# Storing the output by tokens instead of by features, and starting the streamed rows 40 bytes later: one decoder step on one core

## The chip, the core and the metric

One core of a Trainium2 chip runs one inference step of a hybrid decoder layer: 256 prompt tokens and 8 sample tokens go through the same weights in float32. TensorE (PE in the profile) multiplies; its weight loads are shown apart as PEld. VectorE is DVE, ScalarE is ACT, GpSimd is POOL, and SyncE (SP) issues most of the transfers. The metric is the time of one execution on the device in microseconds (us); lower is better.

## The reference

What is computed, cut to what this change touches:

```python
hn = rmsnorm(h, norm_gain)                  # h: 264 tokens (256 + 8) x 4096
P  = hn @ w_in                              # one projection, its columns split into groups
A  = sliding_window_attention(...) * silu(z_a)
B  = mlstm(...)  -> also the states C, n, m
C  = u * (tril(W_s) v + b) * silu(z_c)
h  = h + concat(A, B, C) @ w_out            # 4096 x 4096
y  = h * rsqrt(mean(h*h, -1) + 1e-6) * final_gain
```

The outputs are y for the 256 prompt tokens and for the 8 sample tokens, the new rows of keys and values, and the states.

## The kernel before

Activations lie with features on the 128 partitions and tokens along the row. The 4096 features are `KT` = 32 blocks of 128, the 264 tokens are `T`. `yb` [128, 32, 264] holds the input at first, later the gated mixer outputs, later still the residual and the output.

A float32 product is made from three passes at full precision of the array's fast format: the streamed operand is split into `xh` + `xl`, the weights into `wh` + `wl` (tiles [128, 2, 512], three buffers each), and each block adds `wh·xh`, `wh·xl` and `wl·xh` in PSUM. The streamed operand is always a row of `xh` or `xl`, 264 numbers of 4 bytes. Rows of `xh` and `xl` are `ROW` = 320 numbers (1280 bytes) apart, and both tiles start at an address that is a multiple of 256 bytes, so every row starts at such a multiple; so do the weight tiles.

The main loop walks `steps`, pairs of a group (26 groups of 512 columns of `w_in`, then `NGO` = 8 groups of `w_out`) and one of 16 chunks of two feature blocks. Each step issues a 512 KB weight load four steps ahead (SP's queue), the split of the weights two steps ahead (ACT makes `wh`, DVE `wl`), and 24 matmuls, so a group has 384 and the program 13,056. The schedule is written out by hand: each engine executes its instructions in the order in which the code emits them. Small work of the mixers runs in generators between the matmuls.

After a group of `w_out`, `evac_out(i, ps)` adds the product of output block i to `yb` (DVE), squares it (ACT), adds the square to `acc` (POOL, for all but the last two blocks, which stay apart in the list `last`), and multiplies the block by its column of `final_gain` (ACT).

The tail begins after the last matmul. `state_mm(h)` computes the state of head h in PSUM (two matmuls), `state_out(h)` copies it to `co` (ACT), and three transfers on ACT's queue store it as `o_cp`. `norm_factor` sums the squares over the partitions with an all-ones matrix, so the factor `rstd` appears on all 128 partitions for all 264 tokens: ACT takes the root, and DVE does a reciprocal and three more operations, all [128, 264]. `finish` then multiplies 32 blocks of `yb` by `rstd`, every fourth one on POOL, the others on DVE, and SP stores them with nine transfers as `o_y` [128, 32, 264], features on the partitions.

PSUM is split into pools: `pm` with four buffers (tile `mp`: the main products, and the states in the tail), `px` with three (`mx`), `pn` with one.

Of the kernel before, what the change touches and what calls it, by code (L numbers as in the profile page):

```python
# [10 lines left out]
F32 = mybir.dt.float32  # L11
F32R = mybir.dt.float32r
AF = mybir.ActivationFunctionType
ALU = mybir.AluOpType
# [4 lines left out]
P = 128  # L19
D = 4096  # L20
KT = D // P
TP = 256
TS = 8
T = TP + TS
AH, AKV = 12, 4
MH, DK, DV = 6, 128, 256
# [39 lines left out]
NGO = 8  # L66
# [3 lines left out]
LAG = 6.0  # L70
NCH = KT // KK
ROW = 320
PAD0, PAD1 = 32, 24

SM = {}
# [13 lines left out]


def body(tc, xt, wi, wg, wo, sm, kc, vc, c0, wst, w00, bs, cgain, cbias,
         o_y, o_kv, o_cp, o_mp, o_cs, o_ms, o_cvp, o_cvs):
    nc = tc.nc
    from contextlib import ExitStack
    with ExitStack() as ctx:
        cp = ctx.enter_context(tc.tile_pool(name="const", bufs=1))
        wp = ctx.enter_context(tc.tile_pool(name="wp", bufs=3))
        hp = ctx.enter_context(tc.tile_pool(name="hp", bufs=1))
        dp = ctx.enter_context(tc.tile_pool(name="dp", bufs=1, space=DRAM))
        pm = ctx.enter_context(tc.tile_pool(name="pm", bufs=8 - 1 - NMX, space=PSUM))  # L100
        px = ctx.enter_context(tc.tile_pool(name="px", bufs=NMX, space=PSUM))
        pn = ctx.enter_context(tc.tile_pool(name="pn", bufs=1, space=PSUM))
# [20 lines left out]
        ph = Phase("ph")  # L123
# [1 line left out]
        keep = Phase("keep")  # L125

        cp.tile([P, PAD0], F32, name="pad0")
        xh = cp.tile([P, KT, ROW], F32R, name="xh")[:, :, :T]
        xl = cp.tile([P, KT, ROW], F32R, name="xl")[:, :, :T]
        yb = cp.tile([P, KT, T], F32, name="yb")  # L130
        sms = cp.tile([P, NSM], F32, name="sms")
        ones = cp.tile([P, P], F32, name="ones")
        epsc = cp.tile([P, 2], F32, name="epsc")
        epsc2 = cp.tile([P, 1], F32, name="epsc2")
        rstd = cp.tile([P, T], F32, name="rstd")
        cp.tile([P, PAD1], F32, name="pad1")
        acc = cp.tile([P, KK, T], F32, name="acc")

        def sc(name, i=0, n=None, rows=slice(None)):
            o, w = SM[name]  # L140
            return sms[rows, o + i:o + i + (1 if n is None else n)]
# [9 lines left out]
        def tt(eng, out, a, b, op):  # L151
            eng.tensor_tensor(out, a, b, op)
# [56 lines left out]
        V = Eng(nc.vector, "V", 0.1, 0.00104)  # L209
        A = Eng(nc.scalar, "A", 0.25, 0.00083)  # L210
        G = Eng(nc.gpsimd, "G", 0.15, 0.00228)
        PE = Eng(nc.tensor, "P", 0.0, 0.0)
        DQ = nc.sync
# [62 lines left out]
        def newton(out, v, t):  # L276
            V.reciprocal(out, t)
            tt(V, v, v, out, ALU.mult)
            tt(V, v, v, out, ALU.mult)
            V.scalar_tensor_tensor(out, v, 1.5, out, ALU.add, ALU.mult)  # L280

        def norm_factor(ps, parts):
            for i, a in enumerate(parts):
                PE.matmul(ps[:, :T], ones, a, start=(i == 0), stop=(i == len(parts) - 1))
            v = hp.tile([P, T], F32, name="es", bufs=2)
            t = hp.tile([P, T], F32, name="es", bufs=2)

            A.activation(t, ps[:, :T], AF.Sqrt, scale=1.0 / D, bias=epsc[:, 0:1])
            A.activation(v, ps[:, :T], AF.Identity, scale=-0.5 / D, bias=epsc[:, 1:2])
            newton(rstd, v, t)  # L290
# [361 lines left out]
        def attn_sample_loads():  # L652
            Kc = ph.tile([P, TS, AKV, P], F32, name="Kc", tag="big", bufs=2)
            Vc = ph.tile([P, TS, AKV, P], F32, name="Vc", tag="big", bufs=2)

            def loads():
                for dst, src in ((Kc, kc), (Vc, vc)):
                    for i in range(0, TS, 2):
                        DQ.dma_start(dst[:, i:i + 2], src[:, i:i + 2])
                        yield 4.0  # L660

            spawn(loads(), urgent)
            pad = ph.tile([P, TS, AKV, 32], F32, name="pad")
            prod = ph.tile([P, AKV, 32], F32, name="prod")
            G.memset(pad, 0.0)
            G.memset(prod, 0.0)
            st.update(Kc=Kc, Vc=Vc, pad=pad, prod=prod)
# [258 lines left out]
        def before_group(g):  # L926
            if g < NG:
# [14 lines left out]
                if x == ("aq", 0, O_AQ):  # L942
                    attn_sample_loads()

        def evac_out(i, ps):
            y = yb[:, i]
            tt(V, y, ps, y, ALU.add)
            if i >= KT - 2:
                s = hp.tile([P, T], F32, name="et", bufs=4) if i < KT - 1 else acc[:, 1]
                A.activation(s, y, AF.Square)  # L950
                last.append(s)
            elif i == 0:
                A.activation(acc[:, 0], y, AF.Square)
            else:
                s = hp.tile([P, T], F32, name="es", bufs=2)
                A.activation(s, y, AF.Square)
                tt(G, acc[:, 0], acc[:, 0], s, ALU.add)
            A.activation(y, y, AF.Copy, scale=sc("fg", i))
            if i == 0:
                A.activation(epsc2, epsc[:, 0:1], AF.Sqrt)  # L960

        last = []
# [30 lines left out]
        for n, (g, c) in enumerate(steps):  # L993
# [24 lines left out]
            for j in range(4):  # L1018
                tick()
                out = main_ps[j][:, :T]  # L1020
                for kk in range(KK):
                    k = KK * c + kk
                    s = slice(P * j, P * j + P)
                    PE.matmul(out, wh[:, kk, s], xh[:, k], start=(k == 0), stop=False)
                    PE.matmul(out, wh[:, kk, s], xl[:, k], start=False, stop=False)
                    PE.matmul(out, wl[:, kk, s], xh[:, k], start=False, stop=(k == KT - 1))
                if c == NCH - 1:
                    if g < NG:
                        kind, i, _ = GROUPS[g][j]
                        evac(g, kind, i, out)  # L1030
                    else:
                        evac_out(4 * (g - NG) + j, out)
# [14 lines left out]
        ph.close()  # L1047
        ph.switch()
        co = ph.tile([P, MH, DV + 1], F32, name="co")
        cps = []  # L1050

        def state_mm(h):
            ps = pm.tile([P, 512], F32, name="mp")
            for b in range(2):
                PE.matmul(ps[:, :DV + 1], st["kws"][:, h, b], st["va"][:, h, b], start=(b == 0), stop=(b == 1))
            cps.append(ps)

        def state_out(h):
            A.activation(co[:, h], cps[h][:, :DV + 1], AF.Copy)
            if h in (2, 4, 5):  # L1060
                i = {2: 0, 4: 3, 5: 5}[h]
                nc.scalar.dma_start(o_cp[i:h + 1].rearrange("h p d -> p h d"), co[:, i:h + 1])

        state_mm(0)
        norm_factor(px.tile([P, 512], F32, name="mx"), [acc[:, 0]] + last)
        for h in range(MH):
            if h:
                state_mm(h)
            state_out(h)

        def finish(i, m, sl):
            for k in range(i, i + m):
                tt(G if k % 4 == 3 else V, yb[:, k, sl], yb[:, k, sl], rstd[:, sl], ALU.mult)
            DQ.dma_start(o_y[:, i:i + m, sl], yb[:, i:i + m, sl])

        i = 0
        for m in (2, 4, 4, 4, 4, 4, 4, 4, 2):
            finish(i, m, slice(0, T))
            i += m
        ph.close()  # L1080
        keep.close()


_OUTS = {
    "o_y": (P, KT, T), "o_kv": (2, P, AKV, P + TS), "o_cp": (MH, P, DV + 1), "o_mp": (MH, 1),
    "o_cs": (MH, P, TS, DV + 1), "o_ms": (MH, TS), "o_cvp": (P, 1024), "o_cvs": (TS, 1024),
}

# [91 lines left out]
```

## Time and profile before

| what | value |
|---|---|
| time, median of 3 runs | 1690.13 us (1689.64 to 1691.94) |
| the profiled execution's own time | 1690.53 us |
| its span, first to last instruction | 1687.7 us |
| PE busy | 1663.3 us, 99% of the span |
| DVE, ACT, POOL busy | 911.6, 739.1, 80.9 us |
| moved by DMA | 328.91 MB, 195 GB/s over the span |
| last main matmul starts | 1662.66 us after the span's start |

A line of the profile gives the source line, the engine, the operation, output and inputs by the program's names, shapes, the count, and then busy time and mean duration. All compute instructions of this kernel pass through one helper, so they share one line (L205) and are told apart by the names of their tiles. A matmul's shown duration is longer than the distance to the next one, since matmuls overlap in the array; the rate is read from how many fit in a stretch. A row of a view over stretches ("windows") gives, for each engine, the busy time and in brackets the number of instructions seen in it, then the granted clock of TensorE, the busy share of the 16 DMA engines and the rate.

### The profile page before, as it was taken

To read this page: it belongs to the slowest core of one execution; us is meant where nothing else is said; L and a number is where in the kernel's file an instruction comes from. 1 tells how busy PE (TensorE), PEld (TensorE's weight loads), DVE (VectorE), ACT (ScalarE), POOL (GpSimd) and SP (SyncE) were. 2 spreads that over 40 slices of the span, in tenths; PEclk is the share of its full clock that TensorE was granted. 3 is DMA by queue.
4 is the path that set the end of the run, shared out by engine and by line. 5 is a ranking of instruction groups with operands and counts; after the bars stand their busy time and mean duration, and the time that the engine had idled before them with its cause. 6 is when DMAs were issued, how large, how long until landed. Compare 5 with 4: busy or idle time off the path is not lost.

```text
span 1687.7 us, 32534 instructions
## 1 busy us (share of the span) xinstructions
PE 1663.3 (99%) x13754; PEld 1646.4 (98%) x13754; DVE 911.6 (54%) x1277; ACT 739.1 (44%) x971; POOL 80.9 (5%) x82
## 2 busy tenths in 40 slices
PE   9999999999999999999999999999999999999995
PEld 9999999999999999999999999999999999999995
DVE  6565644555544455556665666444666554444445
ACT  6554433444434343444444444334454444344442
POOL 0000000000000000001001100000100030000002
PEclk9999999999999999999999999999999999999998
DMA  8555568545455555667767666555656656555553
GB/s 297 172 181 178 184 191 278 157 156 165 151 173 178 184 179 184 205 205 234 229 215 241 216 226 214 185 179 185 204 176 224 203 192 192 187 180 184 180 182 147
DMA packets 102177, 328.91 MB, mean 195 GB/s; under 512 B 11090, under 2 KB 24328, under 8 KB 102032
## 3 DMA queue, kind: packets, MB, share of 16 engines
q1 hardware_dynamic: 101072, 326.04, 60.4%
q8 instruction: 107, 1.75, 0.4%
q10 hardware_dynamic: 960, 0.81, 0.1%
q14 instruction: 38, 0.31, 0.0%
HBM read 314.20 MB, written 12.60 MB: 194 GB/s over the span
## 4 chain that ended last, share of the span: by engine, by line
PE 96%; DVE 2%; DMA 1%; ACT 1%; issue 0%; SPq 0%; DVEq 0%; ACTq 0%
PE mp L205 92%; PE mx L205 3%; DVE wl L205 1%; DVE yb L205 1%; DMA wf<-wo 1%; PE sn L205 0%; ACT wh L205 0%; DMA wf<-wi 0%; PE gps L205 0%; DVE rstd L205 0%; DVE TM L205 0%; ACT es L205 0%; DVE mvs L205 0%; ACT L205 0%; ACT yb L205 0%
## 5 line engine op out<-in xcount | busy, mean ns | idle before, releaser
L205 PE MATMUL mp<-xh,wh 128*128 128x264 f32 x4352 | 1242.5, 286 | 2.5 <-ACT wh L205 1.9
L205 PE MATMUL mp<-xh,wl 128*128 128x264 f32 x4352 | 1231.3, 283 | 2.6 <-DVE wl L205 2.5
L205 PE MATMUL mp<-xl,wh 128*128 128x264 f32 x4352 | 1230.9, 283 | 0.0
L205 DVE TENSOR_TENSOR wl<-wf,wh 128x1024 fp32r<-128x1024 f32 (+1 forms) x545 | 685.3, 1261 | 741.1 <-ACT wh L205 734.5
L205 ACT ACTIVATE wh<-wf 128x1024 fp32r<-128x1024 f32 (+1 forms) x545 | 574.9, 1057 | 808.6 <-PE mp L205 712.1
L205 PEld LDWEIGHTS mp<-xh,wh 128*128 128x128 f32 x4352 | 819.0, 188 | 9.3 <-issue 5.6
L205 PEld LDWEIGHTS mp<-xh,wl 128*128 128x128 f32 x4352 | 819.0, 188 | 3.9 <-DVE wl L205 3.9
L205 PEld LDWEIGHTS mp<-xl,wh 128*128 128x128 f32 x4352 | 819.2, 188 | 0.4
L205 POOL TENSOR_TENSOR acc<-acc,es 128x264 f32<-128x264 f32 x29 | 21.9, 756 | 412.4 <-ACT es L205 410.3
L205 ACT ACT_TABLE_LOAD x22 | 28.2, 1283 | 1.2 <-PEq L1160 0.8
L205 POOL TENSOR_SCALAR_AFFINE_SELECT tmp<-bc 128x128 f32<-128x128 f32 x12 | 5.1, 448 | 491.8 <-DMA bc<-gd 446.0
L205 ACT ACTIVATE es<-yb 128x264 f32<-128x264 f32 x37 | 15.2, 412 | 17.7 <-DVE yb L205 17.7
L205 POOL TENSOR_TENSOR cb<-cb,bc 128x2056 f32<-128x2056 f32 x6 | 22.5, 3748 | 0.2 <-PE mx L205 0.2
L205 ACT ACTIVATE bias<-bias,ar 128x128 f32<-128x128 f32 (+1 forms) x24 | 10.7, 448 | 24.9 <-DVE ar L205 24.8
L205 POOL MEMSET pad<- 128x1024 f32 x2 | 1.9, 950 | 409.5 <-PE mx L205 409.5
L205 ACT ACTIVATE es<-et 128x264 f32<-128x264 f32 x32 | 12.6, 419 | 17.1 <-DVE yb L205 13.8
L205 DVE SCALAR_TENSOR_TENSOR cb<-vb,wsk,cb 128x257 f32<-128x257 f32 x48 | 20.1, 481 | 0.0
L205 ACT ACTIVATE xh<-yb 128x264 fp32r<-128x264 f32 x32 | 12.1, 412 | 17.7 <-DVE yb L205 17.7
L205 DVE TENSOR_TENSOR et<-mp,rstd 128x264 f32<-128x264 f32 x52 | 18.8, 424 | 0.0
L205 ACT ACTIVATE yb<-yb,sms 128x264 f32<-128x264 f32 x32 | 16.5, 517 | 1.0
L205 DVE TENSOR_TENSOR yb<-yb,rstd 128x264 f32<-128x264 f32 x32 | 16.1, 559 | 0.0
L205 DVE TENSOR_TENSOR xl<-yb,xh 128x264 fp32r<-128x264 f32 x32 | 12.7, 429 | 3.9 <-ACT xh L205 3.9
(177 smaller groups left out, 467.4 us busy)
## 6 DMA issues: line engine op xcount, KB each, us to landing
wf<-wi SPq DMA_DIRECT2D x415, 512.0 KB, 3.4
wf<-wo SPq DMA_DIRECT2D x128, 512.0 KB, 3.4
cb<-c SPq DMA_DIRECT2D x12, 514.0 KB
o_cs<-cb SPq DMA_DIRECT2D x12, 514.0 KB, 6.3
vb<-vsd SPq DMA_DIRECT2D x12, 512.0 KB, 4.6
yb<-xt SPq DMA_DIRECT2D x34, 132.0 KB, 3.4
yb<-xt SPq DMA_DIRECT2D x15, 264.0 KB, 7.3
o_y<-yb SPq DMA_DIRECT2D x7, 528.0 KB, 3.2
```

The costliest lines, as they stand in the source:

```text
L205: return fn(*a, **k)
```

## The change

Three things change, two of them in the tail.

1. `xh` and `xl` keep their addresses and their pitch, but the 264 numbers now begin 10 numbers (40 bytes) into each row of 320.
2. The norm factor is computed by tokens. For each of the two blocks of 128 tokens, the squares are the stationary operand and one column of ones is streamed, so the sum of a token lands on that token's partition; for the 8 sample tokens the factor stays along the row, as before. One small tile of 10 columns replaces the [128, 264] chain.
3. The output is turned. `turn(q, b)` transposes four feature blocks of token block b in PSUM, [128 tokens, 512 features]. `put(q, b)` multiplies the block by the factor of its token while it leaves PSUM, on ACT for b = 0 and on DVE for b = 1, and SP stores it as 128 rows of 2 KB in `o_y` [2, 128, 4096]. The eight sample tokens go out by one DVE operation and one transfer, `o_ys`. POOL has no part any more. The states move to the pool `px`, and their matmuls, copies and transfers (now three of two heads) are dealt between the turned blocks. Since a block must have its `final_gain` before it is turned, that multiplication of the last three blocks comes later: block 29 after the last square, blocks 30 and 31 between the first turned blocks.

```diff
+XOFF = 10
...
-        xh = cp.tile([P, KT, ROW], F32R, name="xh")[:, :, :T]
-        xl = cp.tile([P, KT, ROW], F32R, name="xl")[:, :, :T]
+        xh = cp.tile([P, KT, ROW], F32R, name="xh")[:, :, XOFF:XOFF + T]
+        xl = cp.tile([P, KT, ROW], F32R, name="xl")[:, :, XOFF:XOFF + T]
...
+        def final_gain(k):
+            A.activation(yb[:, k], yb[:, k], AF.Copy, scale=sc("fg", k))
...
-            A.activation(y, y, AF.Copy, scale=sc("fg", i))
+            if i < KT - 3:
+                final_gain(i)
+            elif i == KT - 1:
+                final_gain(KT - 3)
...
+        def state(h):
+            ps = px.tile([P, 512], F32, name="mx")
...
-        norm_factor(px.tile([P, 512], F32, name="mx"), [acc[:, 0]] + last)
...
-        def finish(i, m, sl):
-            for k in range(i, i + m):
-                tt(G if k % 4 == 3 else V, yb[:, k, sl], yb[:, k, sl], rstd[:, sl], ALU.mult)
-            DQ.dma_start(o_y[:, i:i + m, sl], yb[:, i:i + m, sl])
...
+        def turn(q, b):
+            ps = pm.tile([P, 512], F32, name="mp")
+            for k in range(4):
+                tr(ps[:, P * k:P * k + P], yb[:, 4 * q + k, P * b:P * b + P])
+            turned[q, b] = ps
+        def put(q, b):
+            ps, o = turned.pop((q, b)), yo[:, q, b]
+            if b == 0:
+                A.activation(o, ps, AF.Copy, scale=r[:, 0:1])
+            else:
+                V.tensor_scalar(o, ps, r[:, 1:2], None, ALU.mult)
+            DQ.dma_start(o_y[b, :, 512 * q:512 * q + 512], o)
...
+            for b in range(2):
+                PE.matmul(ns[:, b:b + 1], a[:, P * b:P * b + P], ones[:, 0:1], ...)
+            PE.matmul(ns[:, 2:2 + TS], ones, a[:, TP:], ...)
...
+        rsqrt(r[:, 0], ns[:, :2 + TS], 1.0 / D, r[:, 1], r[:, 2])
...
+        for q in range(NGO):
+            put(q, 0)
+            put(q, 1)
+            if q < MH:
+                state_out(q)
+            if q < 2:
+                final_gain(KT - 2 + q)
+            if q == 2:
+                tt(V, yos, yb[:, :, TP:], rs.unsqueeze(1).broadcast_to([P, KT, TS]), ALU.mult)
+                DQ.dma_start(o_ys, yos)
+            if q + 1 < MH:
+                state(q + 1)
+            if q + 2 < NGO:
+                turn(q + 2, 0)
+                turn(q + 2, 1)
```

How the order on two engines changes in the tail. PE before, from the last matmul of the main loop on (`mp<-va,kws` are states, `ones` against `acc` and `et` is the norm):

```order
L205 MATMUL mp<-xh,wl 128x264
L205 MATMUL mp<-va,kws 128x257 x2
L205 MATMUL mx<-acc,ones 128x264
L205 MATMUL mx<-et,ones 128x264
L205 MATMUL mx<-acc,ones 128x264
L205 MATMUL mp<-va,kws 128x257 x10
```

PE after, the same place (`mp<-sms,yb` are the transposes, whose identity matrix lies in `sms`; the norm is the `ns` rows):

```order
L206 MATMUL mp<-xh,wl 128x264
L206 MATMUL mp<-sms,yb 128x128 x8
L206 MATMUL mx<-va,kws 128x257 x2
L206 MATMUL ns<-ones,acc 128x1 x2
L206 MATMUL ns<-acc,ones 128x8
L206 MATMUL ns<-ones,et 128x1 x2
L206 MATMUL ns<-et,ones 128x8
L206 MATMUL ns<-ones,acc 128x1 x2
L206 MATMUL ns<-acc,ones 128x8
L206 MATMUL mp<-sms,yb 128x128 x8
L206 MATMUL mx<-va,kws 128x257 x2
L206 MATMUL mp<-sms,yb 128x128 x8
```

Eight transposes and nine narrow norm matmuls now stand where three wide norm matmuls stood, and the remaining states alternate with further transposes, 64 of these in all.

ACT before, from the last squares on (`et` and `acc` are the squares of blocks 30 and 31, `yb<-yb,sms` is the final gain):

```order
L205 ACTIVATE et<-yb 128x264
L205 ACTIVATE yb<-yb,sms 128x264
L205 ACTIVATE acc<-yb 128x264
L205 ACTIVATE yb<-yb,sms 128x264
L205 ACTIVATE es<-mx,epsc 128x264 x2
L205 ACTIVATE co<-mp 128x257 x3
L1062 DMA o_cp<-co 128x3x257
```

ACT after, the same place:

```order
L206 ACTIVATE et<-yb 128x264
L206 ACTIVATE acc<-yb 128x264
L206 ACTIVATE yb<-yb,sms 128x264
L206 ACTIVATE rn<-ns,epsc 128x10
L206 ACTIVATE yo<-mp,rn 128x512
L206 ACTIVATE co<-mx 128x257
L206 ACTIVATE yb<-yb,sms 128x264
L206 ACTIVATE yo<-mp,rn 128x512
L206 ACTIVATE co<-mx 128x257
L1070 DMA o_cp<-co 128x2x257
```

The last square no longer stands behind a gain, and ACT now carries eight `yo` blocks between the state copies and two late gains.

More of the change, by code (lines that the diff above doesn't have):

```diff
@@ L91, in body @@
 def body(tc, xt, wi, wg, wo, sm, kc, vc, c0, wst, w00, bs, cgain, cbias,
-         o_y, o_kv, o_cp, o_mp, o_cs, o_ms, o_cvp, o_cvs):
+         o_y, o_ys, o_kv, o_cp, o_mp, o_cs, o_ms, o_cvp, o_cvs):
     nc = tc.nc
@@ L1049, in body @@
         co = ph.tile([P, MH, DV + 1], F32, name="co")
-        cps = []
-        def state_mm(h):
-            ps = pm.tile([P, 512], F32, name="mp")
+        yo = ph.tile([P, NGO, 2, 512], F32, name="yo")
+        yos = ph.tile([P, KT, TS], F32, name="yos")
+        turned, cps = {}, {}
+        def state(h):
+            ps = px.tile([P, 512], F32, name="mx")
+            cps[h] = ps
             for b in range(2):
                 PE.matmul(ps[:, :DV + 1], st["kws"][:, h, b], st["va"][:, h, b], start=(b == 0), stop=(b == 1))
-            cps.append(ps)
@@ L1058, in state_out @@
         def state_out(h):
             A.activation(co[:, h], cps[h][:, :DV + 1], AF.Copy)
[L1060 to L1064, printed above, removed]
-        norm_factor(px.tile([P, 512], F32, name="mx"), [acc[:, 0]] + last)
[L1066 to L1069, printed above, removed]
-        def finish(i, m, sl):
-            for k in range(i, i + m):
-                tt(G if k % 4 == 3 else V, yb[:, k, sl], yb[:, k, sl], rstd[:, sl], ALU.mult)
-            DQ.dma_start(o_y[:, i:i + m, sl], yb[:, i:i + m, sl])
@@ L1076, in body @@
[L1076 to L1079, printed above, removed]
+            if h in (1, 3, 5):
+                nc.scalar.dma_start(o_cp[h - 1:h + 1].rearrange("h p d -> p h d"), co[:, h - 1:h + 1])
+        def turn(q, b):
[10 more added lines that the diff above has]
+            DQ.dma_start(o_y[b, :, 512 * q:512 * q + 512], o)
@@ new lines, in body @@
+        turn(0, 0)
+        turn(0, 1)
+        state(0)
+        ns = pn.tile([P, 512], F32, name="ns", tag="sn")
+        parts = [acc[:, 0]] + last
+        for i, a in enumerate(parts):
+            end = i == len(parts) - 1
+            for b in range(2):
+                PE.matmul(ns[:, b:b + 1], a[:, P * b:P * b + P], ones[:, 0:1], start=(i == 0 and b == 0), stop=end,
+                          skip_group_check=True)
+            PE.matmul(ns[:, 2:2 + TS], ones, a[:, TP:], start=False, stop=end, skip_group_check=True)
@@ new lines, in body @@
+        r = hp.tile([P, 3, 2 + TS], F32, name="rn")
+        rsqrt(r[:, 0], ns[:, :2 + TS], 1.0 / D, r[:, 1], r[:, 2])
+        rs = r[:, 0, 2:]
+        r = r[:, 0]
+        turn(1, 0)
+        turn(1, 1)
+        for q in range(NGO):
[13 more added lines that the diff above has]
+                turn(q + 2, 1)
@@ L1084 @@
 _OUTS = {
-    "o_y": (P, KT, T), "o_kv": (2, P, AKV, P + TS), "o_cp": (MH, P, DV + 1), "o_mp": (MH, 1),
+    "o_y": (2, P, D), "o_ys": (P, KT, TS), "o_kv": (2, P, AKV, P + TS), "o_cp": (MH, P, DV + 1), "o_mp": (MH, 1),
     "o_cs": (MH, P, TS, DV + 1), "o_ms": (MH, TS), "o_cvp": (P, 1024), "o_cvs": (TS, 1024),
@@ L1168 @@
     r = _run(nc, [arrays], core_ids=[0]).results[0]
-    y = r["o_y"].transpose(2, 1, 0).reshape(T, D)
+    y, ys = r["o_y"].reshape(TP, D), r["o_ys"].transpose(2, 1, 0).reshape(TS, D)
     kv = r["o_kv"].transpose(0, 3, 2, 1)
@@ L1172 @@
     return (
-        y[:TP].reshape(1, TP, D), y[TP:].reshape(TS, 1, D),
+        y.reshape(1, TP, D), ys.reshape(TS, 1, D),
         kv[0, :P][None, None], kv[1, :P][None, None],
```

## The prediction

> **What bounds the kernel now.** I read the page first, then the chain of waits, then counts of matmuls in long stretches of the main loop, then the tail instruction by instruction.
>
> ```profile
> span 1687.7 us, 32534 instructions
> PE 1663.3 (99%) x13754; PEld 1646.4 (98%) x13754; DVE 911.6 (54%) x1277; ACT 739.1 (44%) x971; POOL 80.9 (5%) x82
> PE 96%; DVE 2%; DMA 1%; ACT 1%; issue 0%; SPq 0%; DVEq 0%; ACTq 0%
> L205 PE MATMUL mp<-xh,wh 128*128 128x264 f32 x4352 | 1242.5, 286 | 2.5 <-ACT wh L205 1.9
> ...
> L205 PE MATMUL mp<-xh,wl 128*128 128x264 f32 x4352 | 1231.3, 283 | 2.6 <-DVE wl L205 2.5
> L205 PE MATMUL mp<-xl,wh 128*128 128x264 f32 x4352 | 1230.9, 283 | 0.0
> ```
>
> PE carries 96% of the chain that ended last, nearly all of it three groups of 4352 matmuls whose streamed operand is a row of `xh` or `xl`; they wait 5 us in all. So two things can move the time: the distance between those 13,056 matmuls, and the tail, 25 us from the last main matmul (1662.66) to the end. The distance comes from counting (columns: stretch, its length, PE busy and count, PEld, DVE, ACT, POOL, clock, DMA share, GB/s):
>
> ```profile
> 507.00:599.00 92.00, 92.00 (x760) 92.00 (x759) 40.66 (x37) 36.02 (x40) 0.00 (x0) 1.00 0.59 183
> 61.00:108.00 47.00, 47.00 (x394) 47.00 (x393) 28.06 (x30) 25.45 (x34) 0.00 (x0) 1.00 0.56 173
> 1139.00:1184.00 45.00, 45.00 (x373) 45.00 (x373) 20.82 (x20) 18.68 (x21) 0.00 (x0) 1.00 0.59 185
> 1478.00:1518.00 40.00, 40.00 (x335) 40.00 (x335) 17.09 (x15) 17.55 (x22) 2.67 (x4) 1.00 0.58 183
> 1431.00:1471.00 40.00, 40.00 (x332) 40.00 (x332) 17.45 (x16) 17.54 (x21) 3.03 (x4) 1.00 0.59 185
> ```
>
> About two of each count began before the stretch. That leaves 92.00/758 = 121.4 ns in the first, 45.00/371 = 121.3 and 40.00/330 = 121.2 in the third and fifth, but 47.00/392 = 119.9 and 40.00/333 = 120.1 in the second and fourth: the same instructions on the same rows run in two rhythms, whole stretches long, at full clock, whatever DVE and ACT do beside them. I take half the matmuls for each. Now the tail:
>
> ```profile
> 1662.66 0.29 PE L205 MATMUL mp<-xh,wl 128*128 128x264 f32 x1
> 1662.79 1.03 PE L205 MATMUL mp<-va,kws 128*128 128x257 f32 x4
> 1663.66 0.62 PE L205 MATMUL mx<-acc,ones 128*128 128x264 f32 x2
> 1664.11 0.61 PE L205 MATMUL mx<-et,ones 128*128 128x264 f32 x2
> 1664.56 0.61 PE L205 MATMUL mx<-acc,ones 128*128 128x264 f32 x2
> 1665.00 4.51 PE L205 MATMUL mp<-va,kws 128*128 128x257 f32 x20
> 1663.93 0.41 ACT L205 ACTIVATE acc<-yb 128x264 f32<-128x264 f32 x1
> 1665.78 1.80 DVE L205 RECIPROCAL rstd<-es 128x264 f32<-128x264 f32 x1 [2.35 <-ACT es L205]
> 1669.09 12.69 DVE L205 TENSOR_TENSOR yb<-yb,rstd 128x264 f32<-128x264 f32 x24
> 1669.13 7.20 POOL L205 TENSOR_TENSOR yb<-yb,rstd 128x264 f32<-128x264 f32 x8 [5.62 <-DVE rstd L205]
> 1670.44 12.64 SPq L1074 DMA_DIRECT2D o_y<-yb  x9
> 1669.00:1672.00 3.00, 0.51 (x3) 0.11 (x1) 2.97 (x5) 0.45 (x2) 2.87 (x4) 1.00 0.75 271
> 1672.00:1677.00 5.00, 0.00 (x0) 0.00 (x0) 5.00 (x8) 0.00 (x0) 4.34 (x5) 0.74 0.29 118
> 1677.00:1685.00 8.00, 0.00 (x0) 0.00 (x0) 4.78 (x14) 0.00 (x0) 0.00 (x0) 0.50 1.01 402
> 1685.00:1687.70 2.70, 0.00 (x0) 0.00 (x0) 0.00 (x0) 0.00 (x0) 0.00 (x0) 0.50 0.26 99
> ```
>
> The factor is ready when the 24 DVE products begin, 1669.09. While POOL multiplies too, DVE manages 8 in 5 us and the transfers stand at a share of 0.29; once POOL is done they run full, 402 GB/s from 1677 to 1685. So the store is fed too slowly for five microseconds and is then its own bound. From 1677.0 on 8.00 x 402 + 2.70 x 99 GB/s = 3.48 MB moved; at 402 GB/s these end 8.7 us later, at 1685.7, so the end follows the last full transfer by 2.0 us.
>
> **The change, part by part.** *Norm.* PE after the last main matmul (its successor starts at 1662.79) first does eight transposes, one state and then the norm:
>
> ```profile
> 818.92 0.60 PE L205 MATMUL mx<-sms,hn 128*128 128x128 f32 x4
> 819.27 0.37 PE L205 MATMUL mp<-xh,wh 128*128 128x264 f32 x1
> 451.86 0.38 PE L205 MATMUL mx<-ones,prod 128*128 128x1 f32 x2
> 452.11 0.37 PE L205 MATMUL mp<-xh,wh 128*128 128x264 f32 x1
> L205 DVE RECIPROCAL r<-r 128x2 f32<-128x2 f32 x12 | 2.0, 166 | 2.0 <-ACT r L205 1.8
> L205 DVE TENSOR_TENSOR r<-r 128x2 f32<-128x2 f32 x18 | 2.9, 162 | 0.6
> L205 ACT ACTIVATE r<-r,epsc 128x2 f32<-128x2 f32 x6 | 1.8, 295 | 0.1
> L205 ACT ACTIVATE va<-mx 128x512 f32<-128x512 f32 x6 | 3.5, 580 | 0.0
> L205 DVE TENSOR_SCALAR hn<-mx,r 128x256 f32<-128x256 f32 x12 | 5.3, 480 | 0.2
> L205 DVE TENSOR_SCALAR kws<-mx,E 128x128 f32<-128x128 f32 x12 | 3.6, 339 | 0.0
> ```
>
> Four transposes take the array 0.44 us at most (the next matmul starts 0.35 behind the first, overlapping the last), so eight take 0.87: 1663.66. A state takes 0.87 (four passes, 1662.79 to 1663.66 above): 1664.53. The squares of block 31 were done at 1664.34 and come 0.44 sooner, without the gain ahead of them, so they don't hold the norm. Its nine matmuls are two passes each; the 128x1 pair took 0.25 with what followed, so nine take 2.25: 1666.8, and 0.2 for the result to come out, 1667.0. In the chain behind, small operations replace wide ones: a root of 0.30, a reciprocal of 0.17, three of 0.16, and 0.1 to cross engines twice: 1668.1, against 1669.09. One us is won, though PE's part is 1.7 us later than now.
>
> *Blocks.* `put` on ACT costs 0.58, as `va<-mx` of the same shape; on DVE, from 0.34 at 128 and 0.48 at 256 columns, 0.76 at 512. ACT has eight of these (4.6), six state copies of 0.39, two gains of 0.52 and three transfer issues of about 0.4:
>
> ```profile
> 1667.35 0.40 ACTq L1062 DMA_DIRECT2D o_cp<-co  x1
> 1667.81 0.39 ACT L205 ACTIVATE co<-mp 128x257 f32<-128x257 f32 x1 [0.49 <-PE mp L205]
> 1664.37 0.52 ACT L205 ACTIVATE yb<-yb,sms 128x264 f32<-128x264 f32 x1
> o_y<-yb SPq DMA_DIRECT2D x7, 528.0 KB, 3.2
> ```
>
> That is 9.2 us; PE has 14 turns of 0.44 and five states of 0.87, 10.5 us, from 1667.0; DVE 6.1 and 0.5 for the sample tokens (256 columns). A turn must wait until a `put` two rounds back frees one of four PSUM buffers, so PE and ACT hold each other up a little: the last block is ready near 1679. POOL's 7.2 us go, and with them the slow five microseconds of DVE.
>
> *Store.* Bytes: `o_y` 4.19 MB, `o_ys` 0.13, `o_cp` 0.79, in all 5.12 MB, 12.7 us at 402 GB/s. Today `o_cp` is out of the way before `o_y` flows; now it shares the flow. First block ready at 1668.7; issue and start of the flow lie between 0 and 1.9 us behind it (3.2 us from issue to landing, less 1.3 for 528 KB at that rate), I take 1.1: 1669.8. 12.7 us later is 1682.5, later than the last block at 1679, so the store bounds; with the 2.0 us behind it the span ends at 1684.5, **3.2 us sooner**. Bounds: flow at once and never starved, 1683.5 (4.2 sooner); turn, `put` and state of a round one after the other, 0.87 + 0.76 + 0.87 + 0.2 = 2.7 us for eight rounds from 1668.1, and 3.2 to land, 1692.9 (5 us later). I take the first kind, since different engines do them. SP issues 17 transfers instead of 9 at 0.33 us each; only themselves wait behind them. The rows stored become shorter, 2 KB instead of 4.2, which may cost rate: from 1669 to 1672, when `o_cp` with 1 KB rows and the first 2.1 KB rows of `o_y` moved, 271 GB/s took a share of 0.75, so 361 at a full share, and 5.12 MB would need 14.2 us, 1.5 more. The new rows are nearer to the long ones; I take 402.
>
> *The 40 bytes.* No instruction is added, and DVE and ACT write the same lengths. No row of this trace has a streamed fast-format row that starts elsewhere, so the price has no direct row. From above and below: the float32 norm matmuls need six passes over 264 columns from 1663.66 to 1665.00, 223 ns each; half of that, 111.7, is my estimate of what a pass at double rate could take with nothing in its way. The present 120.6 is 8.9 over it, so something stalls each matmul, perhaps the weight load of the next one reading at the same place in the rows, and up to 8.9 x 13,056 = 116 us are there to be won. On the other side a row could need one more piece of memory (rival below). The rows nearest are the two rhythms themselves: the stall is a matter of relative position in time, the trace shows the rhythm of 120.0 as a stable one, and a shifted start can lock all matmuls into it. I take that: (121.4 − 119.9) x 13,056 / 2 = **9.6 us** won.
>
> The Trainium skill speaks against any gain here: "TensorE: Matmul & The Clock Gate", Step-by-step, says that the array has two independent read ports, so that loading the next weights takes nothing from the running matmul. By it the offset is worth 0 and the sum would stop at the tail's 3.2. The trace half disagrees: something takes 8.9 ns of every pass, by my estimate.
>
> *Sum:* 1690.53 (the profiled execution, 0.40 above the median) − 3.2 − 9.6 = 1677.7; against the median 1677.3. I say 1678.
>
> **The rivals.** *Rows anywhere are the same* (0.32): the rhythms stay as they are, and only the tail is left, 1690.1 − 3.2 = 1686.9, on the edge of what can be told apart. For it: float32 passes in the tail over `va`, whose rows start at steps of 4 bytes, keep one pace (24 passes). Against: those run at half rate and have room.
>
> *Slower* (0.24): each row costs a piece of memory more. Rows of 1056 bytes from a multiple of 256 fill whole 16-byte pieces, 66 of them; from 40 they touch 67. One piece of 66 is 120.6/66 = 1.8 ns, x 13,056 = 24 us, so 1690.1 − 3.2 + 23.9 = 1711. It decides from 3.2 us / 13,056 = 0.25 ns a matmul on. Against it: whole stretches are alike on rows of every multiple of 256. (The skill, "SBUF — State Buffer", Door 1, gives 16 bytes as the line of this memory, with a penalty for each access that crosses into a new one; no run here shows it.)
>
> *The stall goes entirely* (inside the 0.44 of gain): 1690.1 − 3.2 − 116 = 1571; halfway, 1629.
>
> **How the numbers follow.** Gain in the matmuls 0.44, none 0.32, loss 0.24. A change under 0.2% (3.4 us) can hardly be told from none in this kernel. The middle case lies at that edge and is halved: faster 0.44 + 0.16, same 0.16, slower 0.24. The range leaves out gains beyond three quarters of the stall (1603) and losses over 2.2 ns (1716), about 2 in 10 together; the likeliest case alone, one rhythm throughout, has 1674 to 1682.
>
> **What would show it.** Counts in 40 us stretches near 335 everywhere support the gain; more than 335 means that more of the stall went; 332 or fewer everywhere is the loss. In the tail: `rn` finished near 1668 on the old scale, no POOL products, 402 GB/s without the hole, last landing some 25 − 3 us behind the last main matmul. I am wrong on the tail if ACT's `yo` rows wait long for PE, and wrong on the rows if all counts stay mixed.

## The result, and the profile after

The changed kernel takes 1715.74 us (median of 4 runs, 1715.45 to 1718.36) where the kernel before took 1689.89 beside it (1689.59 to 1691.94): a ratio of 1.0154, 95% interval 1.0136 to 1.0171. It is 26 us slower, where 12 us of gain were forecast. All times and ratios here and below leave out two disturbed executions, one of the kernel before (1804.82 us, at a granted clock of 0.848) and one with the rows 48 bytes in (3270.15 us). The profiled execution after has a span of 1713.7 us against 1687.7.

The page of after; the last three rows are the three groups of main matmuls:

```profile
span 1713.7 us, 32686 instructions
PE 1700.4 (99%) x13830; PEld 1683.4 (98%) x13830; DVE 901.0 (53%) x1263; ACT 743.4 (43%) x978; POOL 74.0 (4%) x74
PE 96%; DVE 1%; DMA 1%; ACT 1%; issue 0%; SPq 0%; DVEq 0%; ACTq 0%
L206 PE MATMUL mp<-xh,wh 128*128 128x264 f32 x4352 | 1250.6, 287 | 1.1 <-ACT wh L206 0.6
L206 PE MATMUL mp<-xh,wl 128*128 128x264 f32 x4352 | 1241.4, 285 | 3.3 <-DVE wl L206 3.1
L206 PE MATMUL mp<-xl,wh 128*128 128x264 f32 x4352 | 1240.6, 285 | 0.0
```

Nothing new waits: PE is still 96% of the chain, and the three groups wait 1.1 + 3.3 = 4.4 us in all, less than the 5.1 of before. PE is busy for 37 us more: 29 of them up to the last main matmul (1685.75 us against 1656.45), with the same instructions, and 8 in the tail, where it now turns the output. So the matmuls of the loop themselves come at longer intervals, and the counts show it. First before, a long stretch of the output groups, then after, the same stretch and one of the input groups (columns as in the prediction's rows):

```profile
1410.00:1650.00 240.00, 240.00 (x1988) 239.92 (x1987) 107.51 (x103) 104.09 (x123) 15.12 (x20) 1.00 0.58 182
```

```profile
1410.00:1650.00 240.00, 240.00 (x1938) 240.00 (x1937) 106.28 (x102) 102.08 (x123) 15.07 (x20) 1.00 0.56 176
510.00:735.00 225.00, 225.00 (x1817) 225.00 (x1816) 107.61 (x120) 87.21 (x96) 0.00 (x0) 1.00 0.58 181
12.00:45.00 33.00, 33.00 (x277) 33.00 (x276) 25.77 (x39) 23.39 (x39) 1.38 (x4) 1.00 0.90 304
1262.00:1297.00 35.00, 35.00 (x294) 35.00 (x293) 21.67 (x33) 19.44 (x33) 0.00 (x0) 1.00 0.57 173
```

With the two that began before a stretch taken off, before gives 240.00/1986 = 120.8 ns, a mean over both of its rhythms. After gives 240.00/1936 = 124.0 and 225.00/1815 = 124.0, at full clock, and also between matmuls during which DVE and ACT both stand idle. The last two rows give 33.00/275 = 120.0 and 35.00/292 = 119.9: the rhythm of 120 is still there on the shifted rows, in a few stretches. The rhythm of 121.3 is gone; one of 124.0 has come in its place and holds most of the loop. At 124.0 ns, 40 us hold 323 matmuls; the prediction had named 332 or fewer as the sign of the loss.

The tail, instruction by instruction (start, then time to the end; a row with a count above 1 runs from the start of its first instruction to the end of its last, pauses included), and the same time as stretches:

```profile
1691.22 0.28 PE L206 MATMUL mp<-xh,wl 128*128 128x264 f32 x1
1691.34 1.04 PE L206 MATMUL mp<-sms,yb 128*128 128x128 f32 x8
1694.79 0.37 PE L206 MATMUL ns<-acc,ones 128*128 128x8 f32 x2
1696.36 0.17 DVE L206 SCALAR_TENSOR_TENSOR rn<-rn 128x10 f32<-128x10 f32 x1
1696.56 0.69 ACT L206 ACTIVATE yo<-mp,rn 128x512 f32<-128x512 f32 x1 [0.89 <-DVE rn L206]
1697.28 3.93 SPq L1085 DMA_DIRECT2D o_y<-yo  x6
1698.44 0.75 DVE L206 TENSOR_SCALAR yo<-mp,rn 128x512 f32<-128x512 f32 x1 [0.39 <-PE mp L206]
1701.92 8.01 SPq L1085 DMA_DIRECT2D o_y<-yo  x10
1705.40 1.27 ACT L206 ACTIVATE yo<-mp,rn 128x512 f32<-128x512 f32 x2 [0.47 <-PE mp L206]
1705.42 1.62 DVE L206 TENSOR_SCALAR yo<-mp,rn 128x512 f32<-128x512 f32 x2 [0.99 <-PE mp L206]
```

```profile
1698.00:1702.00 4.00, 4.00 (x30) 3.66 (x29) 2.00 (x5) 3.07 (x8) 0.00 (x0) 1.00 1.00 357
1702.00:1707.00 5.00, 4.25 (x32) 3.72 (x30) 2.89 (x4) 3.35 (x6) 0.00 (x0) 1.00 1.03 363
1707.00:1712.00 5.00, 0.00 (x0) 0.00 (x0) 0.04 (x1) 0.00 (x0) 0.00 (x0) 0.96 1.01 373
1712.00:1713.70 1.70, 0.00 (x0) 0.00 (x0) 0.00 (x0) 0.00 (x0) 0.00 (x0) 0.50 0.02 7
```

The last main matmul starts at 1691.22, 28.6 us later than before; from there to the end it takes 1713.7 − 1691.2 = 22.5 us instead of 25.0. So 28.6 us were lost in the main loop, 2.5 won in the tail, and 26.1 remain. The loss spread over the loop is 28,560/13,056 = 2.2 ns a matmul.

### The profile page after: what moved, and what is told of

It is laid out like the page before. It is cut to its first block, busy times and chain, and to the rows that moved or that the text cites. A ratio compares the mean times of both kernels' runs of the same rounds, so it can differ in the third digit from the quotient of the medians.

```text
span 1713.7 us, 32686 instructions
## 1 busy us (share of the span) xinstructions
PE 1700.4 (99%) x13830; PEld 1683.4 (98%) x13830; DVE 901.0 (53%) x1263; ACT 743.4 (43%) x978; POOL 74.0 (4%) x74
## 4 chain that ended last, share of the span: by engine, by line
PE 96%; DVE 1%; DMA 1%; ACT 1%; issue 0%; SPq 0%; DVEq 0%; ACTq 0%
PE mp L206 92%; PE mx L206 3%; DVE wl L206 1%; DMA wf<-wo 1%; PE sn L206 0%; DMA wf<-wi 0%; ACT wh L206 0%; PE gps L206 0%; PE ns L206 0%; DVE TM L206 0%; DVE mvs L206 0%; ACT L206 0%; ACT yb L206 0%; ACT es L206 0%; DVE yb L206 0%
## 5 line engine op out<-in xcount | busy, mean ns | idle before, releaser
L206 DVE SCALAR_TENSOR_TENSOR xl<-yb,sms,xh 128x264 fp32r<-128x264 f32 x32 | 14.4, 490 | 1.3 <-ACT xh L206 1.3
L206 DVE TENSOR_TENSOR xl<-yb,xh 128x264 fp32r<-128x264 f32 x32 | 12.7, 429 | 3.9 <-ACT xh L206 3.9
```

What stands on the lines that cost most here:

```text
L206: return fn(*a, **k)
```

## The experiments

The theory after the result: the 40 bytes alone cause the loss, and the tail gains. Its first rival: the new tail, or what it moves in memory, disturbs the loop. Then the question is what about 40 bytes is slow. Rivals there: a row that covers one more piece of memory; the start of the streamed row itself; or its distance from the weight rows, which PE reads at the same time. For this last one two rows of after speak, the matmul before last and the weight load for the last:

```profile
1691.10 0.28 PE L206 MATMUL mp<-xl,wh 128*128 128x264 f32 x1
1691.10 0.19 PEld L206 LDWEIGHTS mp<-xh,wl 128*128 128x128 f32 x1
```

Each load of 0.19 us begins with the matmul ahead of it, so a weight row and a streamed row are read side by side. In the kernels below, `XOFF` sets where streamed rows begin (4 bytes each) and `PAD1` = 32 instead of 24 moves the weight tiles by 32 bytes, and with them all that is allocated behind `pad1`: the unsplit weights `wf`, `acc` and smaller tiles. Except for the first, all have the new tail. Their rows of a profile are all of the same stretch, 1410 to 1650 us, unless said otherwise, and the time from one matmul to the next is its length over (count − 2). "Distance" below is the one in bytes, from weight row to streamed row.

### The two halves of the change apart

The kernel before with only its rows moved:

```diff
+XOFF = 10
-        xh = cp.tile([P, KT, ROW], F32R, name="xh")[:, :, :T]
-        xl = cp.tile([P, KT, ROW], F32R, name="xl")[:, :, :T]
+        xh = cp.tile([P, KT, ROW], F32R, name="xh")[:, :, XOFF:XOFF + T]
+        xl = cp.tile([P, KT, ROW], F32R, name="xl")[:, :, XOFF:XOFF + T]
```

> The tail of before with the rows 40 bytes later. If the rows alone cost the time: 1690 + 32 = 1719 to 1721 us, matmuls 123 to 124 ns apart on the mean as after the whole change. If the turned output is what slowed the main loop (another order, other buffers): 1690, mean 120.7 ns.

And the changed kernel with its rows back:

```diff
-XOFF = 10
+XOFF = 0
```

> The new tail with the rows at multiples of 256 again. Rows theory: main loop as before (120.7 ns on the mean), 22.5 us from the last main matmul to the end against 25.0, so 1687.4 us, 0.15% faster. Rival (the new tail or code costs the main loop): mean stays over 122 ns, time over 1705.

The rows alone: 1720.86 us (1714.39 to 1721.02), ratio 1.0173 [1.0157, 1.0189]. The tail alone: 1687.02 (1685.67 to 1688.91), ratio 0.9984 [0.9975, 0.9993]. Rows alone, two stretches; then tail alone:

```profile
1410.00:1650.00 240.00, 240.00 (x1938) 240.00 (x1937) 104.91 (x101) 101.53 (x121) 15.10 (x20) 1.00 0.57 179
1110.00:1244.00 134.00, 134.00 (x1118) 133.95 (x1117) 69.57 (x76) 54.13 (x60) 7.38 (x2) 1.00 0.61 191
```

```profile
1410.00:1650.00 240.00, 240.00 (x1989) 239.94 (x1988) 108.11 (x103) 103.45 (x124) 15.11 (x20) 1.00 0.58 182
```

The rows alone give the 124.0 of after, the tail alone the 120.8 of before. So the whole loss is the 40 bytes, and the tail is a gain of 0.16%. The second row shows the other rhythm over 134 us, 134.00/1116 = 120.1 ns. At 124.0 these 1116 matmuls would take 4.4 us more. The profiled run was the one of 1714.39, and the other three took about 1721; had that stretch run at 124.0 in them, this would be most of the difference, but they left no trace.

### Other starts: 32, 48, 64 and 8 bytes

```diff
-XOFF = 10
+XOFF = 8      # and 12, 16, 2 in the three others
```

> Rows start 32 bytes in. Pieces of 16 bytes: 66 touched, no loss, 1687 us. Pieces of 64 bytes: 32 + 1056 = 1088 is 17 pieces as at 0, no loss, 1687 us. Position against the weight rows (any shift away from 0 brings the loss): 1710 to 1716 us, slow rhythm near 124 ns. Pieces of 256 bytes: no loss.

> Rows start 48 bytes in, a multiple of 16. Pieces of 16 bytes: no loss, 1687 us. Pieces of 64 bytes: 48 + 1056 = 1104 needs 18 instead of 17, loss as at 40, 1710 to 1716 us. Position against the weight rows: loss, 1710 to 1716 us.

> Streamed rows 64 bytes in, weights at 0. Memory in pieces of 64 bytes or fewer without regard to the weights: as at 0, 120.8 ns, 1687 us. Relative position with a period of 256: another value than at 0, between 120 and 124 ns, 1680 to 1716 us; with a period of 64: 120.8.

> Streamed rows 8 bytes in. Pieces of 16 bytes: 67 pieces, the full loss as at 40, mean 123 to 124 ns, 1711 to 1716 us. Relative position: a small distance, near the value at 0, 120 to 122 ns, 1680 to 1700 us.

```profile
1410.00:1650.00 240.00, 240.00 (x1965) 240.00 (x1964) 106.85 (x102) 102.86 (x122) 15.10 (x20) 1.00 0.58 180
```

At 32 bytes (the row above): 1703.33 us, 1.0078 [1.0065, 1.0092], 240.00/1963 = 122.3 ns. At 48: 1695.3, 1.0035 [1.0021, 1.0048]. At 64: 1686.97, 0.9987 [0.9977, 0.9997], as at 0. At 8: 1711.8, 1.0133 [1.0113, 1.0153]. A price of one more 16-byte piece is out, since at 32 and 48 a row covers whole pieces and pays all the same. A price of one more 64-byte piece is out too: from 32 a row covers 17 of them, as from 0, and loses; from 48 it covers 18 and loses about half as much. The theory of the distance survives, but its forecasts of the size do not: 32 and 48 were to lose as much as 40 (1710 to 1716 us), and 8 was to stay near the value at 0.

### The start of the row, or its distance from the weights

Both moved by 32 bytes, and the weights alone moved:

```diff
-XOFF = 10
-PAD0, PAD1 = 32, 24
+XOFF = 8      # 0 in the second
+PAD0, PAD1 = 32, 32
```

> Streamed rows and weight rows both 32 bytes off 256 (the tile pad1 ahead of the weight tiles is 8 numbers longer). Relative position theory: the two meet as at 0 and 0, mean 120.7 to 120.9 ns, 1687 us. Absolute position theory (only where the streamed rows lie matters): as with the streamed rows alone at 32, mean 122.2, 1703 us.

> Only the weight rows 32 bytes off 256, streamed rows at 0. Relative position theory: a distance of 32 the other way round, mean not 120.8; 121.5 to 124, 1695 to 1720 us, and a rhythm that differs from 120.0 and 121.3. Absolute position of the streamed rows: as at 0, 120.8 ns, 1687 us.

Both by 32, then the weights alone:

```profile
1410.00:1650.00 240.00, 240.00 (x1988) 239.91 (x1987) 107.32 (x104) 104.15 (x123) 15.17 (x20) 1.00 0.57 181
```

```profile
1410.00:1650.00 240.00, 240.00 (x1998) 239.90 (x1998) 107.76 (x103) 102.87 (x122) 15.09 (x20) 1.00 0.56 177
```

With both at 32 the time is 1686.93, 0.9984 [0.9974, 0.9994], and the count, 1988, is that of the kernel before: the loss at 32 is gone although the rows start where they did. With the weights alone at 32 the time is 1677.87, 0.9932 [0.9912, 0.9951], and the count gives 240.00/1996 = 120.2 with the short pauses between groups in it: the rhythm of 120 nearly throughout. The forecast for a distance other than 0 had the sign wrong here (1695 to 1720 us): a distance can gain as well as lose. So the streamed row's own start isn't the cause; where it lies against the weight rows is, or against what moves with them. No run moves the split weights without `wf` and the other tiles behind `pad1`; that it is the split weights is argued, not shown, from what PE loads beside each streamed row.

If the distance decides, and goes round at 256 bytes, moving the weights on by 32 is moving the rows to 224. Four more starts, 224, 216, 128 and 192:

```diff
-XOFF = 10
+XOFF = 56     # and 54, 32, 48 in the three others
```

> Streamed rows 224 bytes in, weights at 0: 32 bytes behind the weight rows, counted round 256, the distance of the weights-at-32 run (120.0 ns, 1678 us) made with the other operand. Relative position with a period of 256: 120.0 ns in one rhythm, 1676 to 1680 us, 0.6 to 0.8% faster than before. Weight rows at 32 are good for a reason of their own, or the period is 64 (224 is 32 there): 122.2 ns as at 32, 1703 us; or 120.8, 1687 us.

> 216 bytes in, 8 off a multiple of 16, 40 bytes behind the weights. Pieces of 16 bytes add a loss at any start off them (8 and 40 were the worst): 122.5 to 124 ns, 1705 to 1716 us. Distance alone, changing gradually: near the 120.0 at 224, 120 to 121 ns, 1677 to 1690 us.

> 128 bytes in, as far from the weights as a period of 256 allows. Distance with a period of 256: a value of its own, 119 to 122 ns, 1665 to 1703 us. Period of 128: as at 0, rhythms of 120.0 and 121.3, 120.8 on the mean, 1687 us.

> 192 bytes in, 64 behind the weights. Distance with a period of 256: between the 120.0 at 224 and the value at 128; 119 to 121 ns, 1665 to 1690 us. Period of 64 (0 and 64 gave 120.8 both): 120.8 ns, 1687 us.

At 224:

```profile
1410.00:1650.00 240.00, 240.00 (x1998) 239.89 (x1998) 108.09 (x103) 103.11 (x123) 15.11 (x20) 1.00 0.57 178
```

224 gives 1678.25, 0.9926 [0.9913, 0.9938], and the count of the weights moved by 32. 216, eight bytes less, gives 1703.1, 1.0072 [1.0057, 1.0088]. 128 gives 1699.22, 1.0054 [1.0039, 1.0069], so the pattern doesn't repeat at 128, and as 32 and 224 differ, not at 64 either. 192 gives 1680.75, 0.9942 [0.9927, 0.9958].

To see the distance at work where both are moved by unlike amounts, rows at 48 and at 40 against weights at 32:

```diff
-XOFF = 10
-PAD0, PAD1 = 32, 24
+XOFF = 12     # 10 in the second
+PAD0, PAD1 = 32, 32
```

> Streamed rows 48 bytes in, weight tiles 32 bytes on: the distance is 16. If the distance alone sets the rhythm, this is the run with 16 and 0: 120.0 ns a matmul, 1677 us. If the rows' own start does, it is the run with 48 and 0: 121.5 ns, 1696 us.

> The changed kernel's rows at 40 bytes, weight tiles 32 bytes on: the distance is 8. By the distance alone: 122.85 ns and 1712 us, as 8 and 0 gave. By the rows' own start: 123.2 ns and 1716 us, as the changed kernel.

Rows at 48, then rows at 40, both against weights at 32:

```profile
1410.00:1650.00 240.00, 240.00 (x1999) 239.87 (x1998) 107.61 (x103) 103.03 (x122) 15.05 (x20) 1.00 0.60 177
```

```profile
1410.00:1650.00 240.00, 240.00 (x1958) 240.00 (x1957) 107.41 (x103) 104.01 (x124) 15.57 (x21) 1.00 0.60 177
```

Rows at 48 fell from 1695.3 to 1678.12 us (0.994 [0.9923, 0.9957]), the time of a distance of 16 (below), by moving the weights only. Rows at 40 came to 1711.41 (1.0134 [1.0119, 1.0149]), the time of a distance of 8 (1.0133), and 240.00/1956 = 122.7 ns instead of 124.0. The intervals of 1.0134 here and 1.0154 for the changed kernel overlap, and it is the rhythms that tell them apart. Two long stretches of the rows at 8 against weights at 0, then two of the rows at 40 against weights at 32:

```profile
210.00:298.00 88.00, 88.00 (x722) 87.84 (x721) 37.21 (x35) 32.37 (x32) 0.00 (x0) 1.00 0.72 229
1550.00:1684.00 134.00, 134.00 (x1089) 134.00 (x1088) 58.24 (x54) 53.36 (x61) 6.06 (x8) 1.00 0.53 169
```

```profile
614.00:762.00 148.00, 148.00 (x1212) 147.90 (x1211) 76.00 (x88) 59.56 (x67) 4.52 (x4) 1.00 0.65 193
1501.00:1595.00 94.00, 94.00 (x765) 94.00 (x764) 41.05 (x39) 39.87 (x47) 6.05 (x8) 1.00 0.61 180
```

The first pair gives 88.00/720 = 122.2 and 134.00/1087 = 123.3 ns, the second 148.00/1210 = 122.3 and 94.00/763 = 123.2: at a distance of 8 there are the same two rhythms from either start, and neither is one of the changed kernel's 120.0 and 124.0, whose rows also start at 40. In every pair with the same distance the times agree, so the distance from the tiles that `PAD1` moves is shown to be what counts.

### Is there a rule for the distance?

Two were tried: that the price follows the distance smoothly, and that a start off a multiple of 16 has a price of its own.

```diff
-XOFF = 10
+XOFF = 52     # and 55, 4, 6 in the three others: 208, 220, 16 and 24 bytes
```

> The changed kernel with the streamed rows 208 bytes into their 256, a multiple of 16 between 192 (120.22 ns a matmul) and 216 (122.0), which is none. Theory A, the distance alone counts and the price goes smoothly with it: between these two, some 121.4 ns, 1695 us. Theory B, starts off a multiple of 16 bytes pay a price of their own: 208 pays none and stays with 192 and 224 at 120.0 to 120.3 ns, 1677 to 1682 us.

> The changed kernel with the rows 220 bytes in, 4 below 224 (120.03 ns) and no multiple of 16. A: between 216 (122.0) and 224, some 121.0 ns, 1690 us. B: like 216, 122.0 ns, 1703 us.

> The changed kernel with the rows 16 bytes in, between 8 (122.85 ns) and 32 (122.2). A: between these, some 122.6 ns, 1709 us. B: between 0 (120.8) and 32 (122.2), its neighbours among the multiples of 16, some 121.5 ns, 1695 us; then 8 bytes pay about 1.7 ns for being off 16, and 40 bytes (123.2 against 122.2 and 121.5 at 32 and 48) about 1.4.

> Streamed rows 24 bytes in, weights at 0. Theory C, starts 8 past a multiple of 16 are dear (8, 40 and 216 were; 220, which is 12 past, was not): 122 ns or more, 1703 us or more. Rival, a smooth course between 16 (120.0) and 32 (122.2): 121.1 ns, 1692 us.

At 220, at 16 and at 24:

```profile
1410.00:1650.00 240.00, 240.00 (x1999) 239.90 (x1999) 106.87 (x102) 102.74 (x122) 15.08 (x20) 1.00 0.56 176
```

```profile
1410.00:1650.00 240.00, 240.00 (x1999) 239.87 (x1998) 108.10 (x103) 103.16 (x123) 15.04 (x20) 1.00 0.56 178
```

```profile
1410.00:1650.00 240.00, 240.00 (x1965) 240.00 (x1964) 106.49 (x103) 103.06 (x122) 15.13 (x20) 1.00 0.60 179
```

Both rules fell. 208 gave 1682.42 (0.995 [0.9934, 0.9967]), near what the second had said; but 220, which is no multiple of 16, gave 1677.43 (0.9923 [0.9908, 0.9938]); 16, between two slow starts, 1677.27 (0.9921 [0.9907, 0.9936]). 24 gave 1704.82 (1.0096 [1.0081, 1.0111]) and 240.00/1963 = 122.3 ns, as the theory of starts 8 past a multiple of 16 had it. All by distance (rows minus weights, round 256):

| distance, bytes | ratio to before | kernels |
|---|---|---|
| 16 | 0.9921, 0.994 | rows 16; rows 48 with weights 32 |
| 220 | 0.9923 | rows 220 |
| 224 | 0.9926, 0.9932 | rows 224; weights 32 |
| 192, 208 | 0.9942, 0.995 | rows 192; rows 208 |
| 0 | 0.9984, 0.9984 | tail alone; both 32 |
| 64 | 0.9987 | rows 64 |
| 48 | 1.0035 | rows 48 |
| 128 | 1.0054 | rows 128 |
| 216 | 1.0072 | rows 216 |
| 32 | 1.0078 | rows 32 |
| 24 | 1.0096 | rows 24 |
| 8 | 1.0133, 1.0134 | rows 8; rows 40 with weights 32 |
| 40 | 1.0154 | the changed kernel |

All four distances of 8 past a multiple of 16 (8, 24, 40, 216) lose, and by more than nearly all others. Among the multiples of 16 no rule that I can state sorts them. What in the memory or in the array makes one distance dear stays open: no view of the profile shows the reads.

## Why the prediction was wrong

**The step that failed** is the one on the 40 bytes: "a shifted start can lock all matmuls into it", priced at 9.6 us of gain with a chance of 0.44. Its first half holds. There are rhythms, and kernels locked into the one of 120.0 exist: the weights moved by 32 took 1677.87 us and the rows at 224, 1678.25, where the prediction said 1678 for that case. But a shift also sets which rhythms there are: 120.0 and 124.0 at a distance of 40, 122.2 and 123.3 at 8, and at 32 a single one near 122.2 (327 or 328 matmuls in each of seven stretches of 40 us). The step took the two rhythms of before as the only two, so it could see 121.4 as the worst; at 40 bytes the slow one is 124.0, and most of the loop fell into it. Neither direction nor size could be read from the trace of before, which holds one distance only. The row chosen as the nearest was therefore no bound, and the loss deserved at least the chance of the gain: of the other distances tried, five gained, one made no difference and six lost. (By the figures in its own brackets the term is 9.8 us, not 9.6, which changes nothing here.)

**The stall of 8.9 ns.** The estimate set 111.7 ns as what a matmul could take with nothing in its way. No run went below 120.0 in a long stretch, and the distances of 16, 220 and 224 all end there (240.00/1997 = 120.2 with the pauses). So nothing shows that the stall exists as something a placement can remove; only the 0.8 between 120.8 and 120.0 was to be had by the placements tried here, and the low end of the range, 1603, had nothing but the estimate behind it; with the tail's 3.2 us it would have been 1600. The high end, 1716, lies just above the measured 1715.74 by luck: no row gave the 2.2 ns a matmul behind it.

**The rival that forecast a loss** gave 1711 and was 5 us off, but it came this near for the wrong reason. Its extra 16-byte piece would cost the same 24 us at 8, 24, 40, 216 and 220, and nothing at 32, 48 or 128. At 220 there was a gain, and at 32, 48 and 128 a loss. What it had right is that the price lies in each of 13,056 matmuls, 2.2 ns instead of 1.8.

**The rules of the Trainium skill.** The time changes with nothing but where the weight rows, and what moves with them, lie against the streamed ones: 1687.02 to 1677.87 by 32 bytes in `PAD1`. The Trainium skill, "TensorE: Matmul & The Clock Gate", Step-by-step, has two independent read ports and loading that takes nothing from the running matmul. The runs do not bear out what the prediction drew from that, an offset worth 0 (1686.9 us against the measured 1715.74); which of the two reads gives way, if either does, no run shows. The Trainium skill, "SBUF — State Buffer", Door 1, has a 16-byte line and a price for crossing into a new one. Four slow distances of 8 past a multiple of 16 may go with it, but 220 fast and 32 slow do not.

**The tail**, 3.2 us forecast and 2.5 measured in the profiled pair; alone it is a ratio of 0.9984, some 2.7 us (interval 1.2 to 4.2). By its steps, with 28.6 taken off for the later start:

- Norm: `rn` finished at 1696.36 + 0.17 = 1696.53, which is 1667.9 on the old scale; 1668.1 was said.
- Blocks: DVE's `put` took 0.75 (0.76 said), ACT's 0.69 (0.58 said, from a copy of the same shape without a scale per token). The last ones end at 1705.42 + 1.62 = 1707.04 (1678.4 on the old scale, 1679 said), some five us ahead of the store's end, so blocks were not the bound, as said.
- POOL's products are gone, and the hole in the transfers with them: the share is 1.00 or more from 1698 to 1712.
- SP's 16 issues of `o_y` took 0.33 to 0.89 us each, 0.55 in the middle, instead of 0.33. With the share at 1.00 or more, this cost nothing that can be seen.
- The term mis-sized was the rate of the store. 357 x 4 + 363 x 5 + 373 x 5 + 7 x 1.7 = 5.12 MB, the bytes forecast, took 14 us, where 402 GB/s would have needed 12.7. The bound quoted beside it, 361 GB/s from rows of 1 and 2.1 KB, was the right row and was passed over for the rate of the 4.2 KB rows. The flow began by 1698.0 (1669.4 on the old scale, 1669.8 said), and the last 1.7 us stand where 2.0 were allowed; these gave part of it back, 1.3 − 0.4 − 0.3 = 0.6 us of the 0.7 that the tail fell short.

## What to carry to other kernels

When the same matmuls run in two rhythms in one trace at full clock, the placement of the operands is worth an experiment, and its sign can't be told from one trace: move streamed and weight rows against each other by a few tens of bytes and count matmuls in a long stretch. A shift that is one number in the code, repeated in 13,056 instructions, outweighed a rebuilt tail by more than ten to one. The changed kernel with its rows at 224 bytes instead of 40, or with 16, has both gains: 1678.25 us and 1677.27 us, ratios of 0.9926 and 0.9921, better than the kernel before and the changed one.

## What the runs showed of the hardware

- The time from one matmul of 264 columns to the next, loads of other weights between them, ran from 120.0 to 124.0 ns at the full granted clock (1.00), by nothing but the distance in bytes between streamed rows and weight rows (with the tiles that move along with these). The same distance made from other addresses gave the same time (0: 1687.02 and 1686.93; 8: 1711.8 and 1711.41; 16: 1677.27 and 1678.12; 224: 1678.25 and 1677.87).
- At one distance there can be two stable rhythms, and a stretch keeps the one it falls into: 120.1 over 134 us and 124.0 over 240 us in one run of the rows alone. The distance sets them: at 8 bytes they were 122.2 and 123.3 in one kernel, 122.3 and 123.2 in another with other addresses.
- Stores with the DMA engines busy throughout moved 357 to 373 GB/s here in rows of 2 KB, with 0.9 of the 5.12 MB in rows of 1 KB; rows of 4.2 KB moved 402.
